# Scores and softmax of the grouped and memory heads, moved ahead of the gate's products

## The chip, the core and the metric

The kernel runs on one core of a Trainium2 chip. The metric is device time in microseconds (us), the median of several executions. A core has engines that each work their own queue in order and meet through semaphores: TensorE (PE in the profile; PEld are its weight loads) multiplies, VectorE (DVE) and ScalarE (ACT) work on elements, GpSimd (POOL) and SyncE (SP) mostly issue transfers here. TensorE writes to PSUM, the other engines drain it to SBUF.

## What is computed

Four decoder layers with 256 tokens and a width of 2048, layers 0 to 3 being latent attention, sparse attention, sliding-window attention and latent attention again. Each layer is one projection into the mixer's streams, memory queries and a gate, then the heads, then the gate and the output projection:

```python
for i in range(DEPTH):
    h = _rmsnorm(x, norm_in[i])
    kind, j = i % N_MIXERS, i // N_MIXERS
    ...
    mem_out = _memory_attention(mq, mem_n @ w_mem_kv[i])
    y = jnp.concatenate([self_out, mem_out], axis=-1) * jax.nn.silu(gate)
    x = x + y @ w_out[i]
```

The sparse and the window layer have 32 heads of 64 features in 4 groups that share keys and values; their logits get a bias by relative position, and in the sparse layer the keys that an indexer did not select get -1e30. The memory heads are 4 heads of 256 features over 256 memory rows.

## The kernel before

All weights come from HBM in fp32 and are used once. A pair of engines splits each 128x512 block of weights into a hi part `wh` (ScalarE, L61) and a lo part `wl` (VectorE, L70), and TensorE makes three products where one would do (hi by hi, lo by hi, hi by lo). `columns_by` (L276, L280) makes features by tokens: for each of 16 k-tiles two 512-wide products with `wh` and two 256-wide ones with `wl`. `rows_by` (L256 to L258) makes tokens by features, with six 512-wide products a k-tile. Accumulators have the tag "acc" and four PSUM buffers, of which each call takes two; everything else in PSUM has the tag "mp" (`misc`), four buffers too.

A layer works in six parts, in the order memory part 4, the self heads' parts 0 to 3, memory part 5. A part of the grouped layers (`Grouped`) is one group of 8 heads: the query projection (two calls of `columns_by`), the gate's 512 columns (`gate`, two calls, so 128 products), the heads, the weighted sums and the gating, and then the output projection `w_out` of the part before (it is `pending`).

The heads of a part are four *pairs* (`head_pair`): four score products `sp` (L966), a bias addition and a min-reduction for each (L974, L975), the exponential (L977), a reciprocal (L988), four normalising copies `u<-u,rc` (L61), then five transposes `ptp` and `pte` (L1000, L1002) and three or four copies of them into `pT`. In the sparse layer the bias is first added to the selection, into a tile `bs` (L972). The memory heads do the same with `msp`, `e` and `ptp` (L584 to L598).

The gate drains an accumulator with `total`: ScalarE copies one half to `z`, VectorE adds the other (L309); then `hz` (L494), `th` (L496) and `gT` (L497). `z`, `hz` and `bs` come from one pool of three buffers, `th`, `e` and `u` from one of four:

```python
z = wk.tile([P, S], F32, name=name, tag="z", bufs=3)
hz = wk.tile([P, S], F32, name="hz", tag="z", bufs=3)
bs = wk.tile([P, S], F32, name="bs", tag="z", bufs=3)
u = wk.tile([P, S], F32, name="u", tag="e", bufs=4)
```

The order on each engine is not written by hand. A scheduler places the instructions at build time; what stands earlier in the program goes first among what it holds to be ready, the weight splits are moved ahead (`high_priority`), and a buffer goes to whoever stands first in the program.

Of the kernel before, what the change touches and what calls it, by code (L numbers as in the profile page):

```python
# [8 lines left out]
F32 = mybir.dt.float32  # L9
# [6 lines left out]
P = 128  # L16
HALF = 64
S = 256
# [14 lines left out]
def kernel(ctx: ExitStack, tc: tile.TileContext, a: dict, out: bass.AP,  # L33
# [10 lines left out]
    def misc(name, dt=F32):  # L44
        return ps.tile([P, 512], dt, name=name, tag="mp", bufs=4)
# [4 lines left out]
    def small(name, n, dt=F32, bufs=None):  # L50
        return wk.tile([P, n], dt, name=name, tag=f"s{n}" if bufs is None else name,
                       bufs=bufs or 6)
# [455 lines left out]
    def normalized(e, r, n):  # L508
        copy_act(e[:, :n], e[:, :n], scale=r)

    def weights_T(es, blocks):

        tp = misc("ptp")
        for i, (b, k) in enumerate(blocks):
            nc.tensor.transpose(tp[:, i * P:(i + 1) * P], es[b][:, k * P:(k + 1) * P], ident)
        return tp
# [38 lines left out]
    def memory_project(nm, i, w, mq0, g0, part, behind):  # L555
        kT, qT = [], []
        if part == 0:
            not_before(behind)
        v = [act.tile([P, 2, 512], F32R, name="mvr", tag="aux", bufs=AUX) for z in range(2)]
        pin = tc.keep_in_program_order if part == 0 else lambda inst: inst  # L560
        for z in range(2):
            pin(nc.gpsimd.dma_start(v[z], mv[i][part][:, z]))
        for h in range(2):
            k = act.tile([P, 2, 2, S], F32R, name="mkr", tag="pq", bufs=PQ)
            pin(nc.gpsimd.dma_start(k, mkT[i][2 * part + h]))
            kT.append(k)
            acc = columns_by(nm.at, 16, w, 0, (mq0 + part * 512 + h * 256, 256), "mq")
            q = act.tile([P, 2, 2, S], F32R, name="mqT", tag="pq", bufs=PQ)
            head_parts(q, acc)
            qT.append(q)  # L570
        return nm, kT, v, qT, gate(nm, w, g0 + 2048 + part * 512)

    def memory_attend(nm, kT, v, qT, gT):
        y = act.tile([P, 2, 4, S], F32R, name="y", tag="y", bufs=2)
        for h in range(2):
            es = []
            mn, sm = small("mn", 2), small("sm", 2)
            for b in range(2):
                sp = misc("msp")
                qs = slice(b * P, (b + 1) * P)  # L580
                seq = [(qT[h][:, u, k, qs], kT[h][:, v_, k, :])
                       for k in range(2) for u, v_ in ((0, 0), (0, 1), (1, 0))]
                for n_, (l, r_) in enumerate(seq):
                    nc.tensor.matmul(sp[:, :S], l, r_, start=n_ == 0, stop=n_ == len(seq) - 1)  # L584
                nc.vector.tensor_reduce(mn[:, b:b + 1], sp[:, :S], AX.X, OP.max, negate=True)
                ms = small("ms", 2)
                nc.vector.tensor_mul(ms[:, :1], mn[:, b:b + 1], nm.col("rstd", b))
                e = wk.tile([P, S], F32, name="e", tag="e", bufs=4)
                nc.scalar.activation(e, sp[:, :S], AF.Exp, bias=ms[:, :1], scale=nm.col("rstd", b),
                                     accum_out=sm[:, b:b + 1])  # L590
                es.append(e)
            r = small("rc", 2)
            nc.vector.reciprocal(r, sm)
            for b in range(2):
                normalized(es[b], r[:, b:b + 1], S)
            tp = weights_T(es, [(0, 0), (1, 0), (0, 1), (1, 1)])
            pH, pL = (wk.tile([P, 768], F32R, name="pT", tag="pT", bufs=PT)[:, :512] for z in range(2))
            split(pH, pL, tp)  # L598
            o = misc("mo")
            for j in range(2):  # L600
                c = (2 * h + j) * P
                seq = [(v[z][:, t, c:c + P], p_[:, t * S:(t + 1) * S])
                       for t in range(2) for z, p_ in ((0, pH), (0, pL), (1, pH))]
                for n_, (l, r_) in enumerate(seq):
                    nc.tensor.matmul(o[:, j * S:(j + 1) * S], l, r_, start=n_ == 0, stop=n_ == 5)
            gated(y, o, gT, 2 * h)
        return y
# [147 lines left out]
    class Grouped:  # L755
# [147 lines left out]
        def project(self, g):  # L903
            nm = self.nm
            q = [act.tile([P, 2, 4, 2, HALF], F32R, name="qS", tag="pq", bufs=PQ) for z in range(2)]
            for z in range(2):
                acc = columns_by(nm.at, 16, self.w, 0, (g * 512 + z * S, S), "q")
                self.heads_by_columns(q[z], acc)
            bm = act.tile([P, 2, 2, S], F32, name="bm", tag=f"big{3 - g % 2}")
            tab = tabs[0 if self.sparse else 1][g]  # L910
            for j in range(2):
                for z in range(2):
                    nc.gpsimd.dma_start(
                        bm[j * HALF:(j + 1) * HALF, z],
                        bass.AP(tensor=tab.tensor, offset=tab.offset + HALF - 1 + (4 * z + 2 * j) * N_TAB,
                                ap=[[8 * N_TAB - 1, HALF], [N_TAB, 2], [1, S]]))
            return g, q, bm, gate(nm, self.w, self.g0 + g * 512)

        def attend(self, g, q, bm, gT):
            while steps:  # L920
                other_work()
            y = act.tile([P, 2, 4, S], F32R, name="y", tag="y", bufs=2)
            pT = [[self.head_pair(g, z, e, q[z][:, e], bm[:, z, e]) for e in range(2)] for z in range(2)]
            for z in range(2):
                o = misc("o")
                for t in range(2):
                    for e in (1, 0):
                        tc.keep_in_program_order(nc.tensor.matmul(
                            o[HALF * e:HALF * e + HALF, t * P:t * P + (512, S)[t]],
                            self.v[:, t, g * HALF:(g + 1) * HALF],  # L930
                            pT[z][e][:, (S, 0)[t]:(768, S)[t]], start=t == 0, stop=t == 1))
                yt = tmp("yt")
                y4 = yt.rearrange("p (j q c) -> p q j c", j=2, q=4)
                o4 = o.rearrange("p (q j c) -> p q j c", q=4, j=2)
                g4 = gT[:, 2 * z:2 * z + 2, :].rearrange("p j (q c) -> p q j c", q=4)
                for j in range(2):
                    nc.vector.tensor_mul(y4[:, 1:, j], o4[:, :3, j], g4[:, 1:, j])
                nc.vector.tensor_mul(y4[:, 0], o4[:, 3], g4[:, 0])
                split(y[:, 0, 2 * z:2 * z + 2, :], y[:, 1, 2 * z:2 * z + 2, :],
                      yt.rearrange("p (a b) -> p a b", a=2))  # L940
            return y
# [214 lines left out]
    for i in range(depth):  # L1156
        kind = kinds[i]
        mixer = Latent(nm, i, kinds[:i].count(0)) if kind == 0 else Grouped(nm, i, kind == 1)
        mixer.first()
        if i == depth - 1:  # L1160
            steps.append(split_ahead(a["w_out"][i], 5))
        nxt = Norm(i + 1) if i + 1 < depth else None

        def w_out(part, y, last):
            for c in range(4):
                acc = rows_by([y], 4, a["w_out"][i], part * 4, (c * 512, 512), "wo")
                for t in range(2):
                    xs = x[t][:, c * 512:(c + 1) * 512]
                    nc.vector.tensor_add(xs, xs, acc[t])  # L1169
                if c == 0 and copies:  # L1170

                    not_before(xs[:, :1])
                    table_copies(*copies.pop(0))
                if last and nxt is not None:
                    nxt.chunk(c)

        pending = None
        order = [4, 0, 1, 2, 3, 5]
        for n_, part in enumerate(order):
            if part >= 4:  # L1180
                y = memory_attend(*memory_project(nm, i, mixer.w, mixer.mq0, mixer.g0, part - 4,
                                                  f32(mixer.k[:, 0] if kind else mixer.kr)[:, 0, :1]))
            else:
                y = mixer.attend(*mixer.project(part))
            if pending is not None:
                w_out(*pending, False)
            pending = (part, y)
        if nxt is None:
            last_out(a["w_out"][i], *pending)
        else:  # L1190
            w_out(*pending, True)
            nxt.finish()
            nm = nxt
# [64 lines left out]
```

## Time and profile before

| | us |
|---|---|
| median of three runs | 2559.21 |
| lowest and highest | 2558.75, 2559.3 |
| the profiled execution | 2558.84 |
| its span, from first to last instruction | 2557.1 |

The span is what the views of the profile divide. Busy times overlap between engines; an engine's idle time counts only where another could not go on without it.

### The profile page before, as it was taken

Reading aid. Unit: us, or ns where it says so; the run is one execution under the profiler, and the core shown is the slowest. Engines: PE = TensorE matmul, PEld = TensorE weight load, DVE = VectorE, ACT = ScalarE, POOL = GpSimd, SP = SyncE. Lnnn points to the kernel's source line nnn. Section 1 sums busy time; section 2 is a strip of 40 time slices with the busy share of each in tenths; the row PEclk is TensorE's granted clock in tenths of the full one; section 3 lists DMA queues with packets and bytes.
Section 4 is the critical chain, followed back from the end, with each engine's and each line's share of the span. In section 5 each row is a group of like instructions: output and inputs, shape, how many; then the busy total and the mean of one; then the engine's idle time right before and its main releaser. Section 6 shows DMA issues by size and latency. Waiting matters only on the chain.

```text
span 2557.1 us, 41908 instructions
## 1 busy us (share of the span) xinstructions
PE 2543.9 (99%) x14016; PEld 2184.1 (85%) x14016; DVE 1891.9 (74%) x4186; ACT 1609.9 (63%) x3488; POOL 103.1 (4%) x250
## 2 busy tenths in 40 slices
PE   9999999999999999999999999999999999999998
PEld 8888888888888889888888888888889888888887
DVE  6666667677777787987787776777777777777777
ACT  6556556556656566666776566766766655665655
POOL 1000000000000000000000000000000000000000
PEclk9999999999999999999999999999999999999999
DMA  9888777666666667665666565656555777666664
GB/s 306 255 259 264 244 212 236 185 167 185 186 191 203 190 192 223 184 201 177 182 185 187 158 213 182 183 172 182 176 168 151 235 201 200 194 193 184 212 174 181
DMA packets 476600, 509.53 MB, mean 199 GB/s; under 512 B 69808, under 2 KB 390208, under 8 KB 475232
## 3 DMA queue, kind: packets, MB, share of 16 engines
q1 hardware_dynamic: 460080, 449.71, 59.3%
q0 software_dynamic: 15584, 56.16, 7.0%
q8 instruction: 110, 1.80, 0.3%
q14 instruction: 106, 0.87, 0.1%
q10 hardware_dynamic: 720, 0.98, 0.1%
HBM read 483.61 MB, written 29.46 MB: 201 GB/s over the span
## 4 chain that ended last, share of the span: by engine, by line
PE 99%; DMA 1%; ACT 0%; issue 0%; SPq 0%; DVE 0%; POOL 0%; POOLq 0%; ACTq 0%
PE acc_g L276 14%; PE acc_g L280 7%; PE acc_wo L257 7%; PE acc_wo L258 7%; PE acc_wo L256 7%; PE acc_mk L276 5%; PE acc_q L276 5%; PE acc_mq L276 4%; PE acc_cq L276 4%; PE acc_qn L276 3%; PE acc_q L280 2%; PE acc_mk L280 2%; PE acc_mv L257 2%; PE acc_mv L256 2%; PE acc_mv L258 2%; PE acc_mq L280 2%
## 5 line engine op out<-in xcount | busy, mean ns | idle before, releaser
L70 DVE TENSOR_TENSOR wl<-wr,wh 128x512 fp32r<-128x512 f32 (+1 forms) x1712 | 1158.5, 680 | 589.7 <-ACT wh L61 561.3
L61 ACT ACTIVATE wh<-wr 128x512 fp32r<-128x512 f32 (+1 forms) x1712 | 1063.3, 623 | 811.8 <-PE acc_g L276 192.5
L276 PE MATMUL acc_g<-xT,wh 128*128 128x512 f32 x1536 | 484.9, 396 | 0.0
L280 PEld LDWEIGHTS acc_g<-xT,wl 128*128 128x128 f32 x1536 | 285.6, 188 | 65.6 <-issue 1.2
L280 PE MATMUL acc_g<-xT,wl 128*128 128x256 f32 x1536 | 303.4, 279 | 0.0
L257 PE MATMUL acc_wo<-wl,y 128*128 128x512 f32 x752 | 295.6, 393 | 0.0
L258 PE MATMUL acc_wo<-wh,y 128*128 128x512 f32 x752 | 292.8, 390 | 0.0
L276 PEld LDWEIGHTS acc_g<-xT,wh 128*128 128x128 f32 x1536 | 236.3, 189 | 6.4 <-ACT pT L61 3.1
L256 PE MATMUL acc_wo<-wh,y 128*128 128x512 f32 x752 | 235.2, 393 | 2.5 <-ACT wh L61 2.5
L257 PEld LDWEIGHTS acc_wo<-wl,y 128*128 128x128 f32 x752 | 141.3, 188 | 29.0
L258 PEld LDWEIGHTS acc_wo<-wh,y 128*128 128x128 f32 x752 | 141.3, 188 | 28.4
L256 PEld LDWEIGHTS acc_wo<-wh,y 128*128 128x128 f32 x752 | 138.0, 188 | 32.1 <-ACT wh L61 5.9
L276 PE MATMUL acc_mq<-xT,wh 128*128 128x512 f32 x512 | 162.2, 397 | 0.0
L276 PE MATMUL acc_mk<-mT,wh 128*128 128x512 f32 x512 | 161.5, 396 | 0.0
L276 PE MATMUL acc_q<-xT,wh 128*128 128x512 f32 x512 | 160.7, 395 | 0.0
L1169 DVE TENSOR_TENSOR x<-x,acc_wo 128x512 f32<-128x512 f32 x184 | 121.3, 682 | 1.4 <-PE acc_wo L258 1.0
L276 PE MATMUL acc_qn<-cT,wh 128*128 128x512 f32 x384 | 121.4, 397 | 0.0
L276 PE MATMUL acc_cq<-xT,wh 128*128 128x512 f32 x384 | 121.0, 396 | 0.0
L280 PEld LDWEIGHTS acc_mk<-mT,wl 128*128 128x128 f32 x512 | 96.1, 188 | 22.8 <-DVE wl L70 0.4
L280 PEld LDWEIGHTS acc_q<-xT,wl 128*128 128x128 f32 x512 | 95.0, 188 | 22.6 <-DVE wl L70 1.3
L280 PEld LDWEIGHTS acc_mq<-xT,wl 128*128 128x128 f32 x512 | 94.1, 188 | 20.0 <-DVE wl L70 0.4
L280 PE MATMUL acc_mq<-xT,wl 128*128 128x256 f32 x512 | 103.7, 281 | 0.0
(323 smaller groups left out, 4178.7 us busy)
## 6 DMA issues: line engine op xcount, KB each, us to landing
wr<-in_w_out_dram SPq DMA_DIRECT2D x188, 512.0 KB, 3.7
wr<-in_w_in_a_dram SPq DMA_DIRECT2D x176, 512.0 KB, 4.3
wr<-in_w_mem_kv_dram SPq DMA_DIRECT2D x120, 512.0 KB, 4.5
wr<-in_w_in_b_dram SPq DMA_DIRECT2D x116, 512.0 KB, 3.6
wr<-in_w_in_c_dram SPq DMA_DIRECT2D x104, 512.0 KB, 3.5
wr<-in_w_uq_dram SPq DMA_DIRECT2D x192, 128.0 KB, 2.6
wr<-in_w_uq_dram SPq DMA_DIRECT2D x48, 256.0 KB, 3.4
wr<-in_w_in_a_dram SPq DMA_DIRECT2D x32, 288.0 KB, 3.0
```

The costliest lines, as they stand in the source:

```text
L61: inst = nc.scalar.activation(o, i, AF.Copy, scale=scale)
L70: nc.vector.tensor_sub(lo, src, f32(hi))
L256: nc.tensor.matmul(acc[t][:, :n], xh, wh[:, :n], start=first, stop=False)
L257: nc.tensor.matmul(acc[t][:, :n], xh, wl[:, :n], start=False, stop=False)
L258: nc.tensor.matmul(acc[t][:, :n], xl, wh[:, :n], start=False, stop=last)
L276: nc.tensor.matmul(acc[j], wh[:, o:o + P], q[:, :, kt % 4, :], start=kt == 0, stop=False)
L280: nc.tensor.matmul(acc[j][:, 0, :], wl[:, o:o + P], q[:, 0, kt % 4, :], start=False, stop=kt == kts - 1)
L1169: nc.vector.tensor_add(xs, xs, acc[t])
```

## The change

In the grouped layers and for the memory heads, everything from the scores to the transposed weights `pT` now stands in the program behind the query projection and ahead of the gate; weighted sums and gating stay behind it. The Latent layers' self heads stay as they are. `memory_attend` becomes `memory_weights` (one head, up to `pT`) and `memory_sums`; `Grouped.attend` goes into `Grouped.project`.

```diff
-        return nm, kT, v, qT, gate(nm, w, g0 + 2048 + part * 512)
-
-    def memory_attend(nm, kT, v, qT, gT):
+        pT = [memory_weights(nm, kT[h], qT[h]) for h in range(2)]
+        return memory_sums(pT, v, gate(nm, w, g0 + 2048 + part * 512))
+
+    def memory_weights(nm, kT, qT):
...
+        pH, pL = (wk.tile([P, 768], F32R, name="pT", tag="pT", bufs=PT)[:, :512] for z in range(2))
+        split(pH, pL, tp)
+        return pH, pL
+
+    def memory_sums(pT, v, gT):
         y = act.tile([P, 2, 4, S], F32R, name="y", tag="y", bufs=2)
         for h in range(2):
...
+            pH, pL = pT[h]
             o = misc("mo")
...
-            return g, q, bm, gate(nm, self.w, self.g0 + g * 512)
-
-        def attend(self, g, q, bm, gT):
             while steps:
                 other_work()
+            pT = [[self.head_pair(g, z, e, q[z][:, e], bm[:, z, e]) for e in range(2)] for z in range(2)]
+            gT = gate(nm, self.w, self.g0 + g * 512)
             y = act.tile([P, 2, 4, S], F32R, name="y", tag="y", bufs=2)
-            pT = [[self.head_pair(g, z, e, q[z][:, e], bm[:, z, e]) for e in range(2)] for z in range(2)]
```

The same instructions run; their order on the engines changes. In the rows of it below a name's number is its buffer, and the bracket names the engines or queues that the instruction waits for.

TensorE before, layer 1, the fourth pair of a middle part: its last score and what stands up to its transposes (the left-out rows are further products of the query projection and the next gate).

```order
L276 MATMUL acc_q_14471<-xT,wh 128x512
L966 MATMUL sp<-kd,qS 128x512 [waits PE_49,Activation_49]
L280 MATMUL acc_q_14470<-xT,wl 128x256 [waits DVE_49]
L280 MATMUL acc_q_14471<-xT,wl 128x256
...
L280 MATMUL acc_g_14592<-xT,wl 128x256
L280 MATMUL acc_g_14593<-xT,wl 128x256
L1000 MATMUL ptp<-ident,u 128x128 [waits PE_49,Activation_49]
L1000 MATMUL ptp<-ident,u 128x128 x3
L1002 MATMUL pte<-ident,u 128x128 [waits PE_49]
L928 MATMUL o<-pT,vs 64x512 [waits PE_49,Pool_49]
```

Between the score `sp` and the transposes `ptp` stand 38 products, 6 of the query projection and 32 of the gate.

TensorE now, layer 1, the third pair of a middle part, in the part's own gate (`acc_g`), up to the output projection (`acc_wo`); the left-out rows are gate products.

```order
L969 MATMUL sp<-kd,qS 128x512 [waits PE_49,Activation_49]
L280 MATMUL acc_g_14012<-xT,wl 128x256
L280 MATMUL acc_g_14013<-xT,wl 128x256
...
L280 MATMUL acc_g_14013<-xT,wl 128x256
L1003 MATMUL ptp<-ident,u 128x128 [waits PE_49,Activation_49]
L1003 MATMUL ptp<-ident,u 128x128 x3
L1005 MATMUL pte<-ident,u 128x128 [waits PE_49]
L969 MATMUL sp<-kd,qS 128x128 [waits DVE_49,PE_49]
L969 MATMUL sp<-kd,qS 128x256 [waits DVE_49,PE_49]
L969 MATMUL sp<-kd,qS 128x384 [waits Activation_49]
L969 MATMUL sp<-kd,qS 128x512 [waits DVE_49,PE_49]
L256 MATMUL acc_wo_14157<-wh,y 128x512 [waits DVE_49]
```

18 gate products are left between score and transposes; the fourth pair's four scores follow, and the output projection's first product waits for VectorE.

TensorE now, part 0 of layer 1, from the end of the gate to the output projection.

```order
L280 MATMUL acc_g_13111<-xT,wl 128x256
L1003 MATMUL ptp<-ident,u 128x128 [waits PE_49,Activation_49]
L1003 MATMUL ptp<-ident,u 128x128 x3
L1005 MATMUL pte<-ident,u 128x128 [waits PE_49]
L969 MATMUL sp<-kd,qS 128x128 [waits PE_49]
L969 MATMUL sp<-kd,qS 128x256 [waits DVE_49,PE_49]
L969 MATMUL sp<-kd,qS 128x384 [waits Activation_49]
L969 MATMUL sp<-kd,qS 128x512 [waits PE_49,Activation_49]
L1003 MATMUL ptp<-ident,u 128x128 [waits DVE_49,PE_49,Activation_49]
L1003 MATMUL ptp<-ident,u 128x128 x3
L1005 MATMUL pte<-ident,u 128x128 [waits DVE_49,PE_49]
...
L256 MATMUL acc_wo_13255<-wh,y 128x512 [waits DVE_49]
```

The second pair's transposes, the third pair's scores and transposes and the fourth pair's scores follow each other with no product between. In the same part the indexer's last scores, which stood in the memory part's gate, now stand in the query projection.

VectorE before, layer 1, where the gate's second half is drained (L309) and the next pair's bias sums `bs` follow.

```order
L309 TENSOR_TENSOR z<-z,acc_g_13812 128x256 [waits Activation_49]
L494 TENSOR_TENSOR hz<-z,half 128x256 [waits DVE_49]
...
L309 TENSOR_TENSOR z<-z,acc_g_13813 128x256 [waits Activation_49]
...
L494 TENSOR_TENSOR hz<-z,half 128x256 [waits DVE_49]
...
L972 TENSOR_TENSOR bs<-bm,sel 128x128 [waits DMASW4_49,DMASW2_49,DVE_49]
L972 TENSOR_TENSOR bs<-bm,sel 128x192 [waits DVE_49]
L974 TENSOR_TENSOR u<-sp,bm 128x64
...
L974 TENSOR_TENSOR u<-sp,bs 128x128 [waits DVE_49]
```

The gate's drains came first, the bias sums after them.

VectorE now, same layer: the fourth pair's additions (L977, which read `sp` and `bs`) and the drain of the gate's first half (L309).

```order
L977 TENSOR_TENSOR u<-sp,bm 128x64 [waits PE_49]
L977 TENSOR_TENSOR u<-sp,bs 128x128 [waits PE_49,Activation_49]
...
L977 TENSOR_TENSOR u<-sp,bs 128x192 [waits PE_49]
L309 TENSOR_TENSOR z<-z,acc_g_13890 128x256 [waits Activation_49]
L977 TENSOR_TENSOR u<-sp,bs 128x256 [waits PE_49]
...
L309 TENSOR_TENSOR z<-z,acc_g_13891 128x256 [waits Activation_49]
```

The drain of the gate's first half now stands behind the fourth pair's additions.

## Rows read from the trace of the kernel before

**Rows 1.** The page: the span, and TensorE's busy time in it.

```profile
span 2557.1 us, 41908 instructions
...
PE 2543.9 (99%) x14016; PEld 2184.1 (85%) x14016; DVE 1891.9 (74%) x4186; ACT 1609.9 (63%) x3488; POOL 103.1 (4%) x250
```

**Rows 2.** PE timeline, first and last; window: columns as in [rows 4].

```profile
1.10 3.92 PE L103 MATMUL wu<-ones 128*128 128x128 f32 x18 [1.10 <-DVE ones L99]
...
2549.22 0.28 PE L1036 MATMUL acc_wo<-wk,y 128*128 128x256 f32 x1
...
2540.00:2557.00 17.00, 9.49 (x54) 8.16 (x52) 9.76 (x29) 7.78 (x20) 0.00 (x0) 0.92 0.32 123
```

**Rows 3.** Waits of PE: us in total, times, longest.

```profile
PE acc_wo L256 <- ACT wh L61: 2.5, 8, 0.3
```

**Rows 4.** Windows, layers 1, 2: us, busy PE, PEld, DVE, ACT, POOL; PEclk.

```profile
905.00:1415.00 510.00, 508.25 (x2835) 434.07 (x2834) 410.27 (x981) 345.70 (x802) 25.38 (x69) 1.00 0.64 192
1512.00:1958.00 446.00, 444.26 (x2448) 375.14 (x2447) 337.24 (x780) 298.66 (x712) 16.28 (x62) 1.00 0.58 177
```

**Rows 5.** Timeline of PE at a wait in layer 1: start, us, what.

```profile
1205.15 0.62 PE L256 MATMUL acc_wo<-wh,y 128*128 128x512 f32 x2
...
1206.51 0.62 PE L256 MATMUL acc_wo<-wh,y 128*128 128x512 f32 x2
...
1210.59 0.61 PE L256 MATMUL acc_wo<-wh,y 128*128 128x512 f32 x2
1211.52 0.73 PE L256 MATMUL acc_wo<-wh,y 128*128 128x512 f32 x2 [0.32 <-ACT wh L61]
```

**Rows 6.** PE timeline, layer 1, a second pair's score, then a fourth pair.

```profile
1149.39 0.56 PE L966 MATMUL sp<-kd,qS 128*128 128x384 f32 x2
...
1174.49 0.39 PE L966 MATMUL sp<-kd,qS 128*128 128x512 f32 x1
...
1176.34 0.63 PE L276 MATMUL acc_g<-xT,wh 128*128 128x512 f32 x2
...
1177.04 0.62 PE L276 MATMUL acc_g<-xT,wh 128*128 128x512 f32 x2
```

**Rows 7.** Timeline of DVE (VectorE) at the same fourth pair.

```profile
1175.33 0.42 DVE L974 TENSOR_TENSOR u<-sp,bs 128x256 f32<-128x256 f32 x1
1175.78 0.42 DVE L975 CUSTOM_DVE_ANT_0 u<-sp,u 128x256 f32<-128x256 f32 x1
...
1177.60 0.17 DVE L988 RECIPROCAL rc<-sm 128x4 f32<-128x4 f32 x1
```

**Rows 8.** Timeline of ACT (ScalarE): the second pair's copies, then the fourth pair.

```profile
1154.80 1.39 ACT L61 ACTIVATE u<-u,rc 128x64 f32<-128x64 f32 x4 [0.50 <-DVE rc L988]
...
1171.09 0.58 ACT L61 ACTIVATE pT<-ptp 128x512 f32<-128x512 f32 x1
...
1176.86 0.51 ACT L977 ACTIVATE u<-u,mn 128x256 f32<-128x256 f32 x1
...
1177.88 1.38 ACT L61 ACTIVATE u<-u,rc 128x64 f32<-128x64 f32 x4
```

**Rows 9.** Timeline of ACT and DVE where a gate half is drained, layer 1.

```profile
1191.70 0.39 ACT L61 ACTIVATE z<-acc_g 128x256 f32<-128x256 f32 x1
...
1192.32 0.41 DVE L309 TENSOR_TENSOR z<-z,acc_g 128x256 f32<-128x256 f32 x1
```

**Rows 10.** Tile bs: count, duration ns min/median/max, first and last start us.

```profile
L972 DVE TENSOR_TENSOR bs<-bm,sel x48: 280/354/428, 1131.5 to 1391.3; 128x128 f32<-128x128 f32 x16, 128x192 f32<-128x192 f32 x16, 128x256 f32<-128x256 f32 x16
```

**Rows 11.** Timeline, layer 2, third pair: last scores (PE), normalising copies (ACT).

```profile
1712.09 0.51 PE L966 MATMUL sp<-kd,qS 128*128 128x384 f32 x2
...
1719.01 1.32 ACT L61 ACTIVATE u<-u,rc 128x64 f32<-128x64 f32 x4
```

**Rows 12.** Timeline, layer 0, memory head: scores (PE), normalising copies (ACT).

```profile
516.44 1.59 PE L584 MATMUL msp<-mkr,mqT 128*128 128x256 f32 x12
...
521.20 0.89 ACT L61 ACTIVATE e<-e,rc 128x256 f32<-128x256 f32 x2
```

More of the change, by code (lines that the diff above doesn't have):

```diff
@@ L570, in memory_project @@
             qT.append(q)
-        return nm, kT, v, qT, gate(nm, w, g0 + 2048 + part * 512)
-    def memory_attend(nm, kT, v, qT, gT):
+        pT = [memory_weights(nm, kT[h], qT[h]) for h in range(2)]
+        return memory_sums(pT, v, gate(nm, w, g0 + 2048 + part * 512))
+    def memory_weights(nm, kT, qT):
+        es = []
+        mn, sm = small("mn", 2), small("sm", 2)
+        for b in range(2):
+            sp = misc("msp")
+            qs = slice(b * P, (b + 1) * P)
+            seq = [(qT[:, u, k, qs], kT[:, v_, k, :])
+                   for k in range(2) for u, v_ in ((0, 0), (0, 1), (1, 0))]
+            for n_, (l, r_) in enumerate(seq):
+                nc.tensor.matmul(sp[:, :S], l, r_, start=n_ == 0, stop=n_ == len(seq) - 1)
+            nc.vector.tensor_reduce(mn[:, b:b + 1], sp[:, :S], AX.X, OP.max, negate=True)
+            ms = small("ms", 2)
+            nc.vector.tensor_mul(ms[:, :1], mn[:, b:b + 1], nm.col("rstd", b))
+            e = wk.tile([P, S], F32, name="e", tag="e", bufs=4)
+            nc.scalar.activation(e, sp[:, :S], AF.Exp, bias=ms[:, :1], scale=nm.col("rstd", b),
+                                 accum_out=sm[:, b:b + 1])
+            es.append(e)
+        r = small("rc", 2)
+        nc.vector.reciprocal(r, sm)
+        for b in range(2):
+            normalized(es[b], r[:, b:b + 1], S)
+        tp = weights_T(es, [(0, 0), (1, 0), (0, 1), (1, 1)])
+        pH, pL = (wk.tile([P, 768], F32R, name="pT", tag="pT", bufs=PT)[:, :512] for z in range(2))
+        split(pH, pL, tp)
+        return pH, pL
@@ L574, in memory_attend @@
+    def memory_sums(pT, v, gT):
         y = act.tile([P, 2, 4, S], F32R, name="y", tag="y", bufs=2)
         for h in range(2):
[L576 to L598, printed above, removed]
+            pH, pL = pT[h]
             o = misc("mo")
@@ L1180 @@
             if part >= 4:
-                y = memory_attend(*memory_project(nm, i, mixer.w, mixer.mq0, mixer.g0, part - 4,
-                                                  f32(mixer.k[:, 0] if kind else mixer.kr)[:, 0, :1]))
+                y = memory_project(nm, i, mixer.w, mixer.mq0, mixer.g0, part - 4,
+                                   f32(mixer.k[:, 0] if kind else mixer.kr)[:, 0, :1])
+            elif kind:
+                y = mixer.project(part)
             else:
```

## The prediction

> **What bounds the kernel now.** I began with the page: TensorE is busy for 2543.9 of 2557.1 us [rows 1]. So the reader first asks where the 13 us of idle time lie. The profiled execution took 2558.84 us, 1.74 us more than its span, and the median of the runs shown is 2559.21 us, 0.37 us above it; I add differences to the median. Of the idle time about 8 us lie at the end: the last matmul starts at 2549.22 us [rows 2]. The waits of TensorE say what is left in the middle: the first product of a pair in the output projection waits 8 times for the hi part of its weight rows, 2.5 us in all [rows 3]. By stage, all idle time lies in two: 1.75 us in layer 1 (sparse attention) and 1.74 us in layer 2 (sliding window) [rows 4]. Both are the layers whose grouped heads this change moves. The Latent layers and the memory rows have none.
>
> A wait costs a little more than its idle time. At 1210.59 us two products start, and the next pair starts at 1211.52; undisturbed products of this kind stand 0.227 us apart (six from 1205.15 to 1206.51), so the pair should have started at 1211.04: 0.48 us are lost, and about 0.12 us more behind it [rows 5]. So 8 such waits cost 8 x 0.6 = 4.8 us, and that is the most that any order of the same work can win in the middle of the kernel. By it the best time is 2554.4 us.
>
> The Trainium skill ("Perfetto Trace Analysis", section Identifying the Most-Contended Engine) warns that the busy share of matmuls is no measure of the distance from the peak; by that rule a reordering might win more than the idle time. The rows do not bear it out for this change: products keep the same pitch (0.227 us, or 0.70 us for the four of a gate step) whatever stands beside them [rows 5, 6].
>
> **The change: what moves.** No instruction is added or removed; 128 scores and 160 transposes of the grouped heads, and the memory heads' work, stand elsewhere. In layer 1 a part has four head pairs. A pair is four scores, on VectorE a bias addition and a min-reduction for each, on ScalarE the exponential, a reciprocal, four normalising copies (u<-u,rc), and then five transposes. Before, these chains were spread over the output projection, the next part's query projection and its gate; now they are squeezed into the part's own gate and the start of the output projection behind it. What matters is how much TensorE work stands between a pair's last score and its transposes, since TensorE works its queue in order and everything behind a waiting transpose waits too.
>
> How long the chain takes is read at the fourth pair of a part: its last score starts at 1174.49 us [rows 6], the addition at 1175.33, the min-reduction at 1175.78, the reciprocal at 1177.60 [rows 7], and the four copies end at 1177.88 + 1.38 = 1179.26 us [rows 8]. That is 4.77 us. Before, 38 products stood there, more than the chain needs, and nothing waited. The second pair's chain is longer: scores at 1149.39 (the second of them 0.16 later), copies until 1154.80 + 1.39 = 1156.19: 6.6 us. With nothing between, the links alone make 0.39 + 0.42 + 0.42 + 0.51 + 0.17 + 1.38 = 3.3 us.
>
> **Parts 1 to 3 of layer 1.** (a) Third pair: 18 gate products stand between last score and transposes. Four take 0.70 us (1176.34 to 1177.04 [rows 6]), so they cover 3.15 us. The chain of 4.77 gives a wait of 1.6 us; the bare one 0.15, the longest 3.45. The new chain holds about the same work of VectorE as the measured one (two weight splits of 0.69 us each, and bias sums where that one has a query addition), so the nearest row should hold; it is the shorter of the two measured, so I lean a little above it: 1.9. (b) Fourth pair: its third score waits until the third pair's transposes have been copied out of PSUM, because `misc` has four buffers and two scores, ptp and pte hold them. The copy is 0.58 us [rows 8], less two short scores: about 0.5 (0 to 0.9). (c) The output projection's first product needs an accumulator. There are four, and the gate's two halves hold all. The first half is drained by z<-acc_g (0.39 us) and the addition behind it (0.41 us) [rows 9], but z shares its three buffers (tag "z") with the bias sums bs, 0.354 us each [rows 10], which in program order now come first. So the drain waits for the fourth pair's scores, as VectorE's order shows. From the second score on: an addition (0.42 at most, [rows 7]), 0.39 and 0.41 make about 1.2 us, less the two scores issued meanwhile: 0.8 (0 to 1.3). (d) The fourth pair's transposes have 18 output products, 18 x 0.227 = 4.1 us, in front, and the wait (c) counts for it too: about 0.2 (0 to 1.2). Sum 3.4 us a part, 10.2 for three; bounds 0.2 and 6.9 a part.
>
> **Part 0 of layer 1.** The selection of keys ends later now (its last scores stand in the query projection), so the pairs come later against the gate, and the third pair's transposes follow its four scores with nothing between: the chain is bare, 4.77 less the score's own 0.39, 4.4 us (2.9 to 6.2). Around it: 0.5 each for the second pair's transposes and for two waits as (b), 1.2 for (c), 0.1 for the rest: 2.8. Sum 7.2 us (4 to 10).
>
> **What goes.** With the chains out of the output projection and the next query projection, weight splits there come in time: the 8 waits go, -4.8 us (0 to -4.8).
>
> **Layer 2.** No bias sums are made, so the gate drains freely. Between a third pair's last score and its transposes stand 2 gate and 27 output products, 0.35 + 6.13 = 6.5 us. Its chain before took from 1712.26 (the second score of the row at 1712.09) to 1719.01 + 1.32 = 1720.33: 8.07 us [rows 11], but with the query's feature work (hl, qS) in between on both engines, which is not there now; the bare links are 3 to 4 us. I take 0.2 us a part for output products that start a little late, 0.8 in all (0 to 4 x 1.6 = 6.4).
>
> **Memory heads.** The second head's chain, from the end of its scores (516.44 + 1.59) to its normalising copies' end (521.20 + 0.89), is 4.1 us [rows 12]; in the new order 32 to 33 gate products, 5.6 us, stand between scores and transposes. Covered: 0; without that cover 4 us a head in eight parts. In the Latent layers nothing else changes. The bias loads (`bm`) of a part are issued far ahead on POOL's queue and no matmul waited for one: 0.
>
> **Sum.** 10.2 + 7.2 - 4.8 + 0.8 = +13.4 us on the profiled 2557.1 + 1.74; against the median 2572.6. The separate small waits tend to overlap (a late first product makes room for the next), so I say 2572 us, slower by 0.5%.
>
> **The rivals.**
> No change: the waits (a) are short because VectorE, relieved of the work around it, runs the chain near its bare 3.3 us. Then parts 1 to 3 lose some 1.5 us each and part 0 some 4.5, and -4.8 comes back: 9.0 + 0.8 - 4.8 = +5 at most, 2559 to 2564 us. Against it: among the rows no chain is under 4.77.
> Not slower, on the other side: the scheduler's order is harmless, since the transposes are ready whenever they come up, and only the 8 waits vanish: 2554.4 us. It needs chains under 3.15 us, below the bare links; and part 0's third pair has no cover at all.
> Harsher: in layer 2 the chain keeps its 8.07 us, and 1.6 us come on top for each of four parts, with fourth pairs and drains late as in layer 1: +6 to +10, 2578 to 2582 us. For it speaks that the row is what it is; against it that the feature work in it has gone.
> The clock: the granted clock is at the upper level (2.4 GHz) throughout and its mean falls to 0.92 only in the last 17 us [rows 2], some time after the last matmul. Whether a wait of 4.4 us in part 0 is enough for a fall to 1.2 GHz, no row shows. If it fell there, the products behind it would run at half speed; I price that with the length of the kernel's first burst of warm-up products, 3.92 us [rows 2], of which half or 2.0 us would be lost: 2574 us. The Trainium skill ("TensorE: Matmul & The Clock Gate", section Why this matters for your kernels) says that gaps between bursts of matmuls bring the lower clock back; the row agrees as far as the clock falls there after the last matmul, and shows it for no gap inside the kernel.
>
> **How the numbers follow.** Forecast (2567 to 2577, the bounds of (a) and part 0 moved half way): 0.65, the clock case 0.04 in it. Harsher: 0.10. Half of the forecast's waits (2564.3 to 2567): 0.12. No change: 0.10. Not slower by the vanished waits: 0.03. A measurement of this kernel can tell about 0.2%, 5.1 us, from no change. The case of the vanished waits, -4.8 us, is at that edge: I give faster 0.02. Slower is 0.65 + 0.10 + 0.12 = 0.87, same 0.11. The range from 2564 to 2579 us leaves out what is unchanged and the worst of the harsher case.
>
> **What would show it.** In the new trace TensorE must wait in layer 1 for ScalarE's u (the normalising copies) before L1003: once some 4 us, three times near 2 us; and before L969 and L256 for pT copies and L309. The waits of L256 for wh must be gone or small. Layer 2 must show no long wait at L1003, and the memory heads none. I am wrong if TensorE's idle time in layer 1 stays under 5 us, or if layer 2 shows waits of over 1 us.

## The result, and the profile after

The changed kernel takes 2578.95 us (median of six, 2578.03 to 2580.16) against 2558.98 us before: a ratio of 1.0079, 95% interval 1.0069 to 1.0089, 20 us slower where 13 were forecast. The page shows first where the 21.3 us between the two profiled spans lie.

```profile
span 2578.4 us, 41933 instructions
...
PE 2554.4 (99%) x14016; PEld 2192.5 (85%) x14016; DVE 1895.9 (74%) x4186; ACT 1612.7 (63%) x3488; POOL 103.3 (4%) x250
```

Beside [rows 1]: the same 14016 products, but TensorE is busy 10.5 us longer (2554.4 against 2543.9) and idle 10.8 us longer (24.0 against 13.2). A new order of the same work should mostly change the idle time. That the busy time rose by as much says that products ran slower, and the reader should look at the clock next. The sign is a rough one: a wait also stretches the busy time around it (in [rows 5] two products take 0.73 us at a wait and 0.62 without), and two of the runs below have the same products, the full clock and 3.2 to 3.5 us less busy time than before. By layer, the windows that answer to [rows 4]:

```profile
905.00:1415.00 510.00, 496.48 (x2688) 420.28 (x2688) 398.68 (x953) 333.70 (x770) 25.44 (x69) 0.98 0.63 183
1512.00:1958.00 446.00, 445.59 (x2450) 376.96 (x2449) 334.05 (x785) 294.40 (x702) 17.87 (x65) 1.00 0.60 182
```

Layer 1 has 13.5 us of idle time and a mean granted clock of 0.98; layer 2 has 0.4 us and 1.00. The waits of TensorE:

```profile
PE ptp L1003 <- ACT u L61: 9.6, 5, 3.7
PE acc_wo L256 <- DVE z L309: 1.8, 4, 0.6
PE sp L969 <- ACT pT L61: 1.6, 4, 0.4
```

The 8 waits for `wh` in the output projection [rows 3] are gone. In their place stand 13 waits of 13.0 us, all in layer 1: the transposes wait for the normalised `u`, the output projection's first product for the gate's drain `z`, the fourth pair's third score for a PSUM buffer. Part 1 of layer 1 on TensorE, from the third pair's last score:

```profile
1210.24 0.39 PE L969 MATMUL sp<-kd,qS 128*128 128x512 f32 x1
...
1213.26 0.39 PE L280 MATMUL acc_g<-xT,wl 128*128 128x256 f32 x2
1215.47 0.66 PE L1003 MATMUL ptp<-ident,u 128*128 128x128 f32 x4 [1.82 <-ACT u L61]
...
1216.87 1.11 PE L969 MATMUL sp<-kd,qS 128*128 128x384 f32 x2 [0.41 <-ACT pT L61]
1218.33 0.80 PE L256 MATMUL acc_wo<-wh,y 128*128 128x512 f32 x1 [0.35 <-DVE z L309]
1218.93 0.63 PE L257 MATMUL acc_wo<-wl,y 128*128 128x512 f32 x1
1219.35 0.63 PE L258 MATMUL acc_wo<-wh,y 128*128 128x512 f32 x1
...
1223.60 0.40 PE L256 MATMUL acc_wo<-wh,y 128*128 128x512 f32 x1
1223.83 0.40 PE L257 MATMUL acc_wo<-wl,y 128*128 128x512 f32 x1
```

The transposes wait 1.82 us, the score 0.41, the first output product 0.35. Behind that look at the pitch, the distance between starts: output products stand 0.42 us apart (1218.93 to 1219.35), and from 1223.60 on 0.23. Windows of 2 us over the same place (busy PE, PEld, DVE, ACT, POOL; PEclk third from the end):

```profile
1214.00:1216.00 2.00, 0.53 (x6) 0.54 (x6) 0.69 (x1) 1.41 (x5) 0.00 (x0) 1.00 0.49 137
1217.00:1219.00 2.00, 1.65 (x4) 0.97 (x5) 1.61 (x8) 1.71 (x8) 2.00 (x4) 0.50 0.42 98
...
1224.00:1226.00 2.00, 2.00 (x12) 1.39 (x13) 1.54 (x3) 2.00 (x6) 0.00 (x0) 1.00 0.00 0
```

The granted clock goes from 1.00 to 0.50, that is from 2.4 to 1.2 GHz, behind the wait, stays there although TensorE is busy again, and comes back. The mean over 0.5 us is below 1.00 from 1216.5 to 1224.0. It falls so in each of the four parts, for some 7 us in three of them and 3.5 in one:

```profile
1134.00:1142.00 8.00, 6.14 (x17) 4.65 (x18) 5.04 (x21) 6.32 (x23) 2.40 (x4) 0.57 0.24 66
1216.00:1224.00 8.00, 7.24 (x21) 5.28 (x19) 5.07 (x21) 5.99 (x21) 2.34 (x4) 0.57 0.34 98
1298.00:1302.00 4.00, 3.44 (x9) 2.53 (x9) 3.87 (x15) 3.87 (x16) 1.95 (x4) 0.58 0.51 131
1376.00:1384.00 8.00, 7.24 (x22) 5.31 (x21) 5.07 (x21) 5.78 (x20) 2.93 (x5) 0.57 0.60 180
```

With the clock at 0.57 or 0.58 over 28 us, 28 x 0.43 = 12 us of full clock are missing; TensorE was busy in 24.06 of the 28 us, so some 24.06 x 0.43 = 10.3 us were lost to products. This estimate is close to the 10.5 us by which the busy time rose.

Part 0 has the bare chain:

```profile
1129.27 0.66 PE L1003 MATMUL ptp<-ident,u 128*128 128x128 f32 x4 [0.44 <-ACT u L61]
...
1130.61 0.94 PE L969 MATMUL sp<-kd,qS 128*128 128x384 f32 x2 [0.35 <-ACT pT L61]
1135.29 1.12 PE L1003 MATMUL ptp<-ident,u 128*128 128x128 f32 x4 [3.73 <-ACT u L61]
...
1138.73 0.79 PE L256 MATMUL acc_wo<-wh,y 128*128 128x512 f32 x1 [0.53 <-DVE z L309]
```

### The profile page after: what moved, and what is told of

It is laid out like the page before. It is cut to its first block, busy times and chain, and to the rows that moved or that the text cites. A ratio compares the mean times of both kernels' runs of the same rounds, so it can differ in the third digit from the quotient of the medians.

```text
span 2578.4 us, 41933 instructions
## 1 busy us (share of the span) xinstructions
PE 2554.4 (99%) x14016; PEld 2192.5 (85%) x14016; DVE 1895.9 (74%) x4186; ACT 1612.7 (63%) x3488; POOL 103.3 (4%) x250
## 4 chain that ended last, share of the span: by engine, by line
PE 98%; ACT 1%; DMA 1%; DVE 0%; issue 0%; SPq 0%; POOL 0%; ACTq 0%; POOLq 0%
PE acc_g L276 14%; PE acc_g L280 7%; PE acc_wo L256 7%; PE acc_wo L257 7%; PE acc_wo L258 7%; PE acc_q L276 5%; PE acc_mk L276 5%; PE acc_mq L276 4%; PE acc_cq L276 3%; PE acc_qn L276 3%; PE acc_mk L280 2%; PE acc_q L280 2%; PE acc_mv L257 2%; PE acc_mv L256 2%; PE acc_mv L258 2%; PE acc_mq L280 2%
## 5 line engine op out<-in xcount | busy, mean ns | idle before, releaser
L258 PE MATMUL acc_wo<-wh,y 128*128 128x512 f32 x752 | 296.1, 394 | 0.0
L256 PE MATMUL acc_wo<-wh,y 128*128 128x512 f32 x752 | 239.7, 397 | 1.8 <-DVE z L309 1.8
```

Of the source, the lines that this page charges most:

```text
L256: nc.tensor.matmul(acc[t][:, :n], xh, wh[:, :n], start=first, stop=False)
L258: nc.tensor.matmul(acc[t][:, :n], xl, wh[:, :n], start=False, stop=last)
```

## The experiments

**One layer at a time.** Only the grouped layer's condition differs; in the second and third run the memory heads' weights are also made where they were before, behind the gate.

```diff
+            gT = None if not self.sparse else gate(nm, self.w, self.g0 + g * 512)
             while steps:
                 other_work()
+            y = None if gT is None else act.tile([P, 2, 4, S], F32R, name="y", tag="y", bufs=2)
             pT = [[self.head_pair(g, z, e, q[z][:, e], bm[:, z, e]) for e in range(2)] for z in range(2)]
-            gT = gate(nm, self.w, self.g0 + g * 512)
-            y = act.tile([P, 2, 4, S], F32R, name="y", tag="y", bufs=2)
+            if gT is None:
+                gT = gate(nm, self.w, self.g0 + g * 512)
+                y = act.tile([P, 2, 4, S], F32R, name="y", tag="y", bufs=2)
```

> Only layer 2's heads and the memory heads stand ahead of the gate; layer 1 is as before. My theory (layer 1 loses twice: waits of 13 us in all, and half clock for some 7 us behind each part's wait, about 10 us more; everything else gains the vanished waits of L256): 2.0 us faster than before, 2557 us, granted clock 1.00 in the kernel's middle, no wait over 0.5 us in layer 2. Rival (the squeezed chains cost something in every layer): no faster than before, 2559 to 2562 us.

2556.90 us against 2559.24: ratio 0.9992 (0.9983 to 1.0001), 2.3 us faster by the medians, though the interval just reaches no change. The clock is 1.00 in every window between 900 and 2540 us, layer 2 has no wait, and of the 8 waits for `wh` four are left, layer 1's:

```profile
PE acc_wo L256 <- ACT wh L61: 1.3, 4, 0.3
```

> Only layer 1's heads stand ahead of the gate; layer 2 and the memory heads are as before. My theory: all of the loss and a little more than in the full change, since layer 2's gain of 2 us is missing: 2580 to 2582 us, with four stretches at 1.2 GHz. Rival (the layers add to each other's loss, through transfers that come late): clearly under 2579 us.

With `self.sparse` in place of `not self.sparse`. 2583.38 us, ratio 1.0095 (1.0081 to 1.0108), 24.1 us slower, a little over what I expected, with four stretches at half clock. All of the loss is layer 1's. Of the 4.4 us to the full change layer 2's gain is 2.3; most of the rest are waits that are longer here: 1.81 us against 0.44 at part 0's second pair, as in the next run, and 2.1 against 1.4 at the kernel's start (`acc_mv`).

> Of the grouped heads only part 0 of layer 1 stands ahead of the gate. My theory: waits of some 5.5 us there (3.7 of them at the third pair's transposes) and one stretch of 7 us at 1.2 GHz, worth 2 to 3 us: 8 to 10 us slower than before, 2567 to 2569 us, one stretch at half clock. Rival (waits alone, the clock costs nothing because TensorE waits in it anyway): 5.5 to 6.5 us slower, 2565 us.

With `self.sparse and g == 0`. 2569.72 us, ratio 1.0041 (1.0028 to 1.0055), 10.5 us slower, a little over the 8 to 10 that I expected. The waits in part 0 are 1.81, 0.35, 3.79 and 0.52 us, 6.5 in all, 1 us more than expected, and the stretch at half clock lasts some 10 us (1134.0 to 1144.2), of which the first 3 are still idle time of the third pair's wait. The rival, in which the clock costs nothing, gave 5.5 to 6.5.

> Only the memory heads stand ahead of the gate; both grouped layers are as before. My theory (a memory head's chain of 4.1 us stands under 5.6 us of gate products, so nothing waits and nothing is won): the same as before within 0.5 us, 2559 us, and the gain of the run with layer 2 and the memory heads comes from layer 2 alone, by the four waits of L256 for wh that vanish there. Rival (the memory heads bring part of that gain): 2558 us or less, with fewer waits in the Latent layers.

With `False`, so that both grouped layers have their old order. 2559.03 against 2559.41 us, ratio 0.9999 (0.9990 to 1.0008): the memory heads are worth nothing either way.

**Filling the waits.** TensorE is given products where it waited, into the tile that the transposes overwrite:

```diff
+            if z == 1 and not swa:
+                if e == 0 and g:
+                    nc.tensor.matmul(tp[:4, :P], mn, ident, start=True, stop=True)
+                for f in range(9 if e else 8 if g else 18):
+                    nc.tensor.matmul(tp, q[:, 0].rearrange("p j c -> p (j c)"),
+                                     self.k[:, g].rearrange("p a b -> p (a b)"), start=True, stop=True)
```

> The full change, and in layer 1 TensorE multiplies where it waited: products of a score's kind into the PSUM tile that the transposes overwrite, 18 ahead of part 0's third pair's transposes, 8 ahead of those of parts 1 to 3 (behind one small product that waits for the min-reduction), and 9 behind each fourth pair's scores: 78 products and 3 small ones, some 18 us of work that the result doesn't need. My theory (idle TensorE brings the clock down): no stretch at 1.2 GHz in layer 1, and the kernel with more work is faster than the changed one: about 2575 us, 4 us under it. Rival (the clock falls for another reason, the small transposes and scores, or VectorE's load): four stretches at 1.2 GHz as before and 4 us more than the changed kernel, 2583 us.

2575.79 us (2575.55 to 2576.53), ratio 1.0066 (1.0051 to 1.0082). All its runs lie under all runs of the changed kernel (2578.03 to 2580.16), although it does more. The page:

```profile
span 2573.7 us, 42113 instructions
...
PE 2563.1 (100%) x14100; PEld 2200.5 (85%) x14100; DVE 1896.7 (74%) x4186; ACT 1609.0 (63%) x3488; POOL 106.4 (4%) x250
```

Part 1 on TensorE, and the window over layer 1's parts:

```profile
1212.09 0.39 PE L280 MATMUL acc_g<-xT,wl 128*128 128x256 f32 x2
1212.41 0.38 PE L1001 MATMUL ptp<-ident,mn 128*4 128x128 f32 x2
1212.72 2.11 PE L1003 MATMUL ptp<-kd,qS 128*128 128x512 f32 x8
1214.67 0.27 PE L1011 MATMUL pte<-ident,u 128*128 128x128 f32 x1
...
1216.27 2.30 PE L1003 MATMUL ptp<-kd,qS 128*128 128x512 f32 x9
1218.41 0.39 PE L256 MATMUL acc_wo<-wh,y 128*128 128x512 f32 x1
```

```profile
1060.00:1460.00 400.00, 399.09 (x2186) 334.37 (x2185) 308.37 (x751) 260.58 (x611) 21.92 (x56) 1.00 0.56 173
```

The 8 products from 1212.72 and the 9 from 1216.27 take the place of the waits, at some 0.24 us each; 78 of them are 18.7 us, and three small ones (0.31 from start to start; the trace counts each as two) 0.9. Without these the busy time is 2563.1 - 19.6 = 2543.5 us, 10.9 under the changed kernel's 2554.4 and close to that of before [rows 1]. So the added busy time vanishes with the idle time, and the rival (the small transposes, or VectorE's load) falls: those are all still there. Of the waits, two of 0.4 and 0.3 us are left in part 0.

> The full change, filled with products only ahead of the third pair's transposes in layer 1 (10 in part 0 and 8 in parts 1 to 3, each behind one small product that waits for the min-reduction), not behind the fourth pair's scores. The transposes then find u ready, the fourth pair's scores follow at once, and the first output product waits longer for z (2.2 us a part, worked out from the durations of the rows), since its drain does not come sooner. My theory (any wait of some 2 us brings the clock down): half clock in each part again, 2581 to 2584 us. Rival (it is the wait at the transposes, or their small products, that brings it down): no stretch at 1.2 GHz in parts 1 to 3, 2574 us or less.

Only the third pair's wait is filled (10 products in part 0, 8 in the others; all four behind the small product). 2576.09 us (2573.90 to 2578.42), ratio 1.0067 (1.0053 to 1.0080): between the two theories. In parts 1 to 3 there is one wait, of 1.54 us at the first output product, not 2.2. Parts 1 and 2 on TensorE, then their windows:

```profile
1220.46 0.52 PE L256 MATMUL acc_wo<-wh,y 128*128 128x512 f32 x1 [1.54 <-DVE z L309]
1220.79 0.61 PE L257 MATMUL acc_wo<-wl,y 128*128 128x512 f32 x1
...
1301.02 0.50 PE L256 MATMUL acc_wo<-wh,y 128*128 128x512 f32 x1 [1.54 <-DVE z L309]
1301.35 0.40 PE L257 MATMUL acc_wo<-wl,y 128*128 128x512 f32 x1
```

```profile
1220.00:1224.00 4.00, 3.54 (x9) 2.82 (x10) 3.12 (x11) 3.23 (x12) 0.50 (x1) 0.60 0.39 105
1301.00:1305.00 4.00, 3.98 (x17) 3.30 (x18) 3.03 (x9) 3.73 (x13) 0.06 (x1) 1.00 0.29 85
```

In part 1 the next product takes 0.61 us (the clock's mean over 4 us is 0.60); in part 2, behind the same wait, 0.40 (1.00). Part 3 is as part 2. In part 0 the clock falls inside a wait of 1.50 us, which the first small product has for the min-reduction behind waits of 0.44 and 0.35; it is back at 1.00 when the first output product waits 1.71 us, and behind this wait it stays up. The runs differ as well: 2573.90, 2574.53 and 2577.66 us had a mean clock of 0.999, and the profiled one, 2578.42, had 0.997, so the others lost less to the clock than this trace shows. So my expectation missed twice: the wait was shorter, and such a wait does not always bring the clock down. The transposes are not needed for a fall: in part 1 they do not wait.

**The shared buffers.** In the changed kernel the first half of the gate, whose 64 products start at 1188.80 us, is drained from 1217.28 us on only, behind the fourth pair's additions that free `bs`. ScalarE (the copies `u<-u,rc` and the drain) and VectorE (the addition, the drain) there:

```profile
1214.04 1.37 ACT L61 ACTIVATE u<-u,rc 128x64 f32<-128x64 f32 x4
...
1217.28 0.39 ACT L61 ACTIVATE z<-acc_g 128x256 f32<-128x256 f32 x1
```

```profile
1216.57 0.29 DVE L977 TENSOR_TENSOR u<-sp,bs 128x128 f32<-128x128 f32 x1
...
1217.87 0.41 DVE L309 TENSOR_TENSOR z<-z,acc_g 128x256 f32<-128x256 f32 x1
```

The products of the output projection have no accumulator until then. So the question is whether they would cover the chains if they had one. `rot` is a tile of the Latent layers of the same size:

```diff
-                    bs = wk.tile([P, S], F32, name="bs", tag="z", bufs=3)
+                    bs = wk.tile([P, S], F32, name="bs", tag="rot", bufs=1)
```

> The full change, and layer 1's bias sums bs get a buffer of their own (that of rot, which only the Latent layers use), so the gate's z and hz no longer queue behind them. My theory (the root of it is the shared buffers: the drain of the gate's first half waits for bs, so no accumulator is free and no product of the output projection can stand under the third and fourth pair's chains): the waits of layer 1 go (under 1 us in all), the clock stays up, the waits of L256 for wh stay away: 2553 us, 6 us faster than before and 26 us faster than the changed kernel. Rival (squeezed chains are too long for any cover there, the buffers only add the 0.4 us at the first output product): some 2 us under the changed kernel, 2577 us, with waits of 1.8 us and half clock as there.

2553.61 against 2558.85 us, ratio 0.9979 (0.9970 to 0.9988): with the one line the change is 5.2 us faster than before, and 25 us faster than as it was made. TensorE's waits are those outside the parts of layer 1:

```profile
PE acc_mv L256 <- ACT wh L61: 1.9, 2, 1.2
PE wu L103 <- DVE ones L99: 1.1, 1, 1.1
PE acc_iq L299 <- ACT wh L61: 0.5, 1, 0.5
```

The window over layer 1's parts has a clock of 1.00 and no more than 0.07 us of idle time:

```profile
1060.00:1460.00 400.00, 399.93 (x2199) 337.93 (x2198) 323.76 (x778) 269.50 (x629) 18.25 (x56) 1.00 0.64 183
```

Part 1 on TensorE from the third pair's last two scores, and ScalarE's drains:

```profile
1200.79 0.56 PE L969 MATMUL sp<-kd,qS 128*128 128x384 f32 x2
...
1204.91 0.62 PE L256 MATMUL acc_wo<-wh,y 128*128 128x512 f32 x2
...
1208.77 0.39 PE L258 MATMUL acc_wo<-wh,y 128*128 128x512 f32 x1
1209.00 0.60 PE L1003 MATMUL ptp<-ident,u 128*128 128x128 f32 x4
```

```profile
1193.25 0.39 ACT L61 ACTIVATE z<-acc_g 128x256 f32<-128x256 f32 x1
...
1195.33 0.36 ACT L61 ACTIVATE z<-acc_g 128x256 f32<-128x256 f32 x1
...
1205.87 1.38 ACT L61 ACTIVATE u<-u,rc 128x64 f32<-128x64 f32 x4
```

The first half's accumulators are drained at 1193.25 and 1195.33, while the second half runs; so output products start at 1204.91, and 18 of them, 4.1 us, stand ahead of the transposes at 1209.00. The copies of `u` ended at 1205.87 + 1.38 = 1207.25: covered, with 1.75 us to spare.

> The kernel before with bs in the buffer of rot, nothing moved. My theory: layer 1's waits of L256 for wh go, since VectorE and ScalarE drain the gate in time; 2 to 5 us faster than before, 2554 to 2557 us. Rival (the shared buffers hurt only where the bias sums stand ahead of the gate): the same as before, 2559 us.

2555.54 against 2558.85 us, ratio 0.9987 (0.9978 to 0.9996), 3.3 us faster. The waits for `wh` that are left are layer 2's:

```profile
PE acc_wo L256 <- ACT wh L61: 1.3, 4, 0.3
```

> As the run with layer 2 and the memory heads moved and layer 1 as before, and bs in the buffer of rot. My theory: the two gains add, 2553 us; against the full change with bs apart it tells what moving layer 1's heads is worth once the buffers are out of the way: within 1 us of it. Rival (moving layer 1's heads is good in itself or bad in itself): 2 us or more apart.

2553.19 us, ratio 0.9977 (0.9967 to 0.9986), 5.7 us faster: the sum of 2.3 and 3.3. It is the best median here, but 0.4 us from the full change with `bs` apart is inside both intervals: once the buffers are out of the way, moving layer 1's heads is worth nothing that these runs can tell.

## Why the prediction was wrong

**The waits: right in kind and near in size.** (a) the third pair was 1.9 us a part, measured 1.82 in each of parts 1 to 3. (b) 0.5, measured 0.41. (c) 0.8, measured 0.35, 0.56 and 0.35. (d) 0.2, measured none. Part 0's bare chain was 4.4, measured 3.73; its other waits 2.8, measured 0.44 + 0.35 + 0.53 = 1.3. In all 17.4 us were forecast and 13.0 of idle time found. The forecast counts from start to start, and by that measure the wait in [rows 5] costs 0.6 us for 0.32 of idle time; with the same 0.28 on each of the 13 waits they make 16.6, an estimate.

**What goes and layer 2: right in kind, small in size.** The 8 waits went. I priced them at 0.6 us each and called 4.8 us the most that any order can win; removing them one layer at a time won 2.3 us (at the edge of its interval) and 3.3, and both together 5.7, 0.7 each and more than that bound. The price is rough, since waits at the kernel's start move from profile to profile too: `acc_mv` has 1.0 us before, where the prediction read none in the memory rows, 0.3 with only the bias sums apart, and 2.1 with part 0 alone. Layer 2's new waits, 0.8 us forecast, did not come. The memory heads cost nothing, as forecast.

**The step that failed is the clock.** I had it as a rival for part 0 alone, with a chance of 0.04, because no row showed a fall inside the kernel, and priced it with 2.0 us, by a burst of products during which the clock stood at 1.00. It fell in all four parts, behind waits of 1.82 us and two smaller ones too, and cost some 10.3 us, more than the whole gap of 7 us between forecast and result. The sum by the corrected terms: 16.6 us of waits, 10.3 of clock, less 5.7 for the vanished ones (as the runs with `bs` apart and layer 1 unmoved have them), makes 21.2; measured 20.0. Against the full change with `bs` apart, which has the order without these waits, the loss is 25.3 us, and 16.6 and 10.3 make 26.9: the estimates are a little high. Without the clock these terms make 10.9, less than the 13 of the forecast. The harsher rival's 2578 to 2582 us holds the measured time, but by luck: its cause, waits in layer 2, did not come (0.4 us of idle time there). That the clock is a cause and not a companion is shown by the filled kernel, in which the waits were filled and the order stayed: it does more, and takes less time.

The Trainium skill ("TensorE: Matmul & The Clock Gate", section A second HAM failure mode: psum-queue depth-cycling) describes a kernel whose TensorE idles briefly but often between groups of products, so that its clock swings between the levels and the products pay for each swing. Part 1's windows agree, with one such swing: three waits of 2.6 us in all, and a stretch at 0.50 behind them. I had weighed the Trainium skill's rule on gaps, as the prediction cites it, against the end of the kernel only, where nothing follows that could show the price.

**What I saw and did not use.** I described that `bs` and `z` share buffers and priced it as term (c), as a wait of 0.8 us. Its larger effect was elsewhere: without an accumulator the output projection could not stand between scores and transposes, so (a) and part 0's wait were consequences of it too. The order showed this: in part 0 and in the third pair's place no `acc_wo` product stands ahead of the transposes. The run with `bs` apart shows it for all of layer 1: the waits, the half clock and the loss go together.

**What stays open.** Why a wait of 1.50 us and one of 1.54 brought the clock down while two more of 1.54 and one of 1.71 did not, and why runs of one kernel differ in it. Also why the clock falls earlier in part 0 when the memory heads are unmoved: 3 us before the third pair's transposes start (1134.0 and 1136.93), against 0.5 in the full change (1134.8 and 1135.29). The longer stretch there, 10 us against 7, is mostly this idle time; its second pair waits 1.81 us, against 0.44 in the full change.

## What to carry to other kernels

Price a wait of TensorE twice: once for its idle time, and once for the clock behind it, at half speed for some microseconds of good work; here the second (10.3 us) was well over half of the first (16.6). It does not come behind every wait, so both cases belong in the range. When a step is moved ahead of another, ask which buffers the two share, and who drains them late: the products that could cover the new wait may be held back by the same buffer. A buffer that sits idle in this phase (here `rot`) can be worth more than the order itself.

## What was not expected of the hardware

The granted clock fell to 1.2 GHz inside a kernel whose TensorE is 99% busy, in three of four places with no single wait over 1.82 us, and most of the time at that level TensorE was at work (24.06 of the 28 us of the windows). Behind one wait of 1.71 us in another run it stayed up. More products made the changed kernel faster: 81 additional ones, 19.6 us of work, and 3 us less time.
